# A new prelude, a deeper stream of loads, and ScalarE copies as seeds of PSUM in place of additions on VectorE

## The chip, the cores and the metric

The kernel runs on one core of a Trainium2 chip. The metric is the device time of one execution in microseconds (us). Times are the median of several runs; a profile is one more execution, recorded by the hardware profiler.

The core has TensorE (PE, matrix products out of SBUF into PSUM; its weight loads are listed as PEld), VectorE (DVE), ScalarE (ACT), GpSimd (POOL), SyncE (SP, which here only issues DMAs) and 16 DMA engines that all queues share. Each engine works through its own instructions in order.

## The reference

One layer of a bidirectional encoder on 512 rows of width 2048, in float32. What matters here is its beginning:

```python
mod = silu(c) @ w_ada + b_ada                    # w_ada: 2048 x 6144
shift, scale, gate = split(mod, 3)
h = rms_norm(x, g) * (1 + scale) + shift         # x: 512 x 2048
proj = h @ w_in                                  # w_in: 2048 x 7168
q_a, k_a, v_a, z_a, q_r, k_r, v_r, z_r = split(proj, ...)
# dilated-window attention (8 heads) on the first four,
# two-way retention (4 heads) on the last four,
# each gated by silu(z), put side by side as y
out = rms_norm(x + gate * (y @ w_out), final_gain)
```

So the product with `w_in` needs h, and a k-tile of h (128 of its 2048 columns) needs the shift and the scale of these 128 columns, and with them 256 columns of all 2048 rows of `w_ada`.

## The kernel before

**Products.** Each float32 operand is split into a high and a low part. For a weight, `conv` (L536 to L552) does it: ScalarE casts the loaded tile `raw` to `whi` (L543), VectorE subtracts to get `wlo` (L544). Each product is then three on TensorE (`mm3`, L85 and L87): high by high, and the two mixed ones.

**The prelude** (L89 to L455) loads, all through SyncE's queue, the columns of `w_ada` for the first k-tile (`araw`, 512-byte rows), then `x` in eight halves of a row tile. VectorE multiplies the 16 pieces of `w_ada` by the entries of silu(c) and adds them (L279, L281). ScalarE squares x (L302), GpSimd takes the power -1/2 of the mean (L319), and x is turned by TensorE and scaled by its rows' factors either in the product itself (L351, with the factors on a diagonal `dg`, L327) or on the way out of PSUM (L373, with the factors spread over all partitions in `rsb`). `psk` holds k-tile 0 of the turned x, from which h of k-tile 0 is made (L385, L386, L389). "Pinned" instructions (`pin`) keep the traced order on their engine; the others are ordered by a planner that goes by the traced order and by when it reckons their inputs to be there.

**Phase 1** (L873 to L974) projects 13 units of 256 columns of `w_in`, with the 16 k-tiles in chunks of 1, 2, 2, 3, 4 and 4 (`CHUNKS`): all units for one chunk, then all for the next, while the modulation of the next chunk is computed. Units 0 and 1 stay in PSUM (`pp`, pool `psP`) through all chunks. The other eleven ("loose") get two banks from a pool of three (`psA`, tile `pw`) for a chunk and are then added to sums in SBUF (`acc`): a copy on ScalarE the first time (L939), an addition on VectorE afterwards (L941). The order of units is turned round from chunk to chunk, and the last loose unit of a chunk stays in PSUM for the next one.

**The modulation of the next chunk** (`ada_pieces`, L188 to L267): steps that load rows of `w_ada` into one of `AR` = 3 buffers `araw` and, `AR` steps later, multiply and add them: the first product on ScalarE (L212), the other 15 on VectorE (L216). Then the sums over the partitions (L230, or turned by TensorE and summed on ScalarE, L244 and L249), shift and scale (L234 to L253), and h: `make_h` on ScalarE (L168, L172) and `make_hl` on VectorE (L181). These steps are put between the items of phase 1 by `plan` (L894), `LAG` = 3 items after the start of the chunk before.

**The stream** (`feed`, L592): an item is half a load of weights. Its load is issued (L564 or L623, buffers `raw`, `RAW` = 3) when it is fed; `LEAD` = 4 items later it is split, and `LOOK` = 2 items after that its products are issued.

The rest of the kernel (attention, retention, the other units, the output projection) isn't touched by the change.

Of the kernel before, what the change touches and what calls it, by code (L numbers as in the profile page):

```python
# [17 lines left out]
P = 128  # L18
D = 2048
# [28 lines left out]
AR = 3  # L48
# [3 lines left out]
def trunk_kernel(ctx, tc, x, c, norm_gain, w_ada, b_ada, w_in, w_out, dec_f, dec_b, final_gain, out):  # L52
# [51 lines left out]
    raw0 = []  # L104
    bg_row = const.tile([48, P], F32, name="bg_row")
    for n in range(4):
        raw = aap.tile([P, 1024], F32, tag="araw" if n < AR else "aacc", name="araw", bufs=AR if n < AR else None)
        rv = raw.rearrange("p (a b f) -> p a b f", a=4, b=2)
        for b in range(2):
            nc.sync.dma_start(  # L110
                rv[:, :, b],
                wa[n * 4 * P : (n + 1) * 4 * P, b * D : b * D + P].rearrange("(a p) f -> p a f", p=P),
            )
            if n + b == 0:
                nc.sync.dma_start(c_row, c.rearrange("b (k p) -> (b k) p", p=P))
        raw0.append(rv)
        if n == 1:
            nc.sync.dma_start(bg_row[0:32, :], b_ada[:, 0 : 2 * D].rearrange("b (k p) -> (b k) p", p=P))
            nc.sync.dma_start(bg_row[32:48, :], norm_gain.rearrange("b (k p) -> (b k) p", p=P))
    ssx = const.tile([P, NT, 2], F32, name="ssx")  # L120
    rsx = const.tile([P, NT], F32, name="rsx")
    xn = []
    for t in range(NT):
        xt = xp.tile([P, D], F32, name=f"xt{t}")
        for h in range(2):
            hs = slice(h * 1024, (h + 1) * 1024)
            nc.sync.dma_start(xt[:, hs], x2[t * P : (t + 1) * P, hs])
# [24 lines left out]
    # an engine keeps to the traced order of pinned instructions  # L152
# [120 lines left out]
    nc.vector.tensor_copy(bg, ps0[:, 64:112])
    nc.vector.tensor_scalar_add(bg[:, 16:32], bg[:, 16:32], 1.0)
    acc0 = [aap.tile([P, 2 * P], F32, tag="acc0", name="acc0") for _ in range(2)]
    for k in range(NK):
        rv, c1 = raw0[k // 4][:, k % 4], ct[:, k : k + 1]
        if k < 2:
            nc.vector.tensor_scalar_mul(acc0[k], rv, c1)  # L279
# [2 lines left out]
    rsb = aap.tile([P, S], F32, name="rsb", bufs=1)

    def sums0():
        psa = bank(psA, "psa")
        for i in range(2):
            for b in range(2):
# [11 lines left out]
    def squares(t, h):
        sq = xp.tile([P, 1024], F32, tag="sq", name="sq")  # L300
        v = xn[t][:, h * 1024 : (h + 1) * 1024]
        marks["sq"] = pin(nc.scalar.activation(sq, v, AF.Square, accum_out=ssx[:, t, h : h + 1]))  # L302

    mss = {}

    def half_root(t):
        ms = mss[t] = small.tile([P, 2], F32, tag="ms2", name="ms2", bufs=2)
        pin(nc.vector.tensor_scalar(ms[:, 0:1], ssx[:, t, 0:1], 1.0 / D, EPS, op0=ALU.mult, op1=ALU.add))

    def roots(t):  # L310
        if t not in mss:
            half_root(t)
        ms = mss[t]
        pin(
            nc.vector.scalar_tensor_tensor(
                ms[:, 1:2], ssx[:, t, 1:2], 1.0 / D, ms[:, 0:1], op0=ALU.mult, op1=ALU.add
            )
        )
        nc.gpsimd.tensor_tensor(rsx[:, t : t + 1], ms[:, 1:2], mhalf[:, 0:1], op=ALU.pow)  # L319

    # the rows' factors: on a diagonal, then on every partition
    dgs = {}
    psbs = {}

    def diagonal(t):
        dg = dgs[t] = xp.tile([P, P], F32, tag="dg", name="dg", bufs=2)
        marks["dg"] = pin(nc.vector.tensor_scalar_mul(dg, ident, rsx[:, t : t + 1]))  # L327
# [979 lines left out]
```

## Time and profile before

| | us |
|---|---|
| median of 3 runs | 971.41 |
| the three runs | 969.67, 971.41, 974.25 |
| span of the profiled execution | 971.6 |

The span runs from the first instruction to the last; of the profiled execution no other time is given. The product of k-tile 0 starts at 28.75 us of the span, chunk 1 at 53.18, chunk 2 at 93.12, chunk 3 at 133.99, chunk 4 at 194.87, chunk 5 at 268.87.

How to read it: a row of a group of instructions gives line, engine, operation, the tile written and the tiles read, the shape, the count, the busy time in us with the mean of one in ns, and the idle time of the engine just before them with what ended most of it. In a timeline the row starts with the start time and the length, and the idle time stands in brackets. In the list of waits: who waited for whom, the total in us, how often, and the longest. Busy time of TensorE isn't progress: a product of 512 columns that ends 0.39 us after its start follows the one before after 0.23 us, so products per stretch say more than the busy share.

### The profile page before, as it was taken

To read this page: it belongs to the slowest core of one execution; us is meant where nothing else is said; L and a number is where in the kernel's file an instruction comes from. 1 tells how busy PE (TensorE), PEld (TensorE's weight loads), DVE (VectorE), ACT (ScalarE), POOL (GpSimd) and SP (SyncE) were. 2 spreads that over 40 slices of the span, in tenths; PEclk is the share of its full clock that TensorE was granted. 3 is DMA by queue.
4 is the path that set the end of the run, shared out by engine and by line. 5 is a ranking of instruction groups with operands and counts; after the bars stand their busy time and mean duration, and the time that the engine had idled before them with its cause. 6 is when DMAs were issued, how large, how long until landed. Compare 5 with 4: busy or idle time off the path is not lost.

```text
span 971.6 us, 14377 instructions
## 1 busy us (share of the span) xinstructions
PE 941.5 (97%) x5556; PEld 820.4 (84%) x5556; DVE 618.0 (64%) x1101; ACT 376.5 (39%) x732; POOL 10.6 (1%) x22
## 2 busy tenths in 40 slices
PE   5989898999999999999999999999999999999996
PEld 4877687788988888988998899988899988888896
DVE  5879978977968786664555556745534382535444
ACT  3824242525235555444343232422333372333321
POOL 0000000000000000000000000000000000000001
PEclk9989999999999999999999999999999999999999
DMA  9786878763552222212224525425322148233304
GB/s 316 232 260 209 270 250 290 266 202 99 183 179 84 65 66 66 65 45 88 84 69 161 186 66 184 143 88 198 126 63 90 57 159 283 86 128 134 109 1 173
DMA packets 109715, 141.49 MB, mean 146 GB/s; under 512 B 6024, under 2 KB 78408, under 8 KB 109648
## 3 DMA queue, kind: packets, MB, share of 16 engines
q1 hardware_dynamic: 108496, 138.49, 43.4%
q10 hardware_dynamic: 1152, 2.10, 0.6%
q8 instruction: 43, 0.70, 0.3%
q14 instruction: 24, 0.20, 0.1%
HBM read 136.36 MB, written 4.20 MB: 145 GB/s over the span
## 4 chain that ended last, share of the span: by engine, by line
PE 89%; DMA 5%; DVE 3%; issue 2%; SPq 1%; ACT 0%; POOLq 0%; POOL 0%; DVEq 0%; ACTq 0%
PE pp L87 26%; PE pw L87 14%; PE pp L85 13%; PE po L87 12%; PE pw L85 7%; PE po L85 6%; PE op L87 3%; PE sp L87 2%; DMA raw<-in_w_in_dram 2%; DMA araw<-in_w_ada_dram 2%; PE op L85 2%; PE tp L770 1%; DVE aacc L216 1%; PE sp L85 1%; DMA xt<-in_x_dram 1%
## 5 line engine op out<-in xcount | busy, mean ns | idle before, releaser
L543 ACT CAST whi<-raw 128x512 fp32r<-128x512 f32 (+1 forms) x289 | 174.9, 606 | 435.8 <-PE pp L87 204.9
L544 DVE TENSOR_TENSOR wlo<-raw,whi 128x512 fp32r<-128x512 f32 (+1 forms) x289 | 193.9, 672 | 209.6 <-ACT whi L543 205.3
L85 PE MATMUL pp<-whi,hh 128*128 128x256 f32 x576 | 162.4, 282 | 0.0
L87 PE MATMUL pp<-wlo,hh 128*128 128x256 f32 x576 | 161.9, 281 | 0.0
L87 PE MATMUL pp<-whi,hl 128*128 128x256 f32 x576 | 161.5, 280 | 0.0
L85 PEld LDWEIGHTS pp<-whi,hh 128*128 128x128 f32 x576 | 108.5, 188 | 2.5 <-ACT sc L839 1.7
L87 PEld LDWEIGHTS pp<-wlo,hh 128*128 128x128 f32 x576 | 108.5, 188 | 1.0 <-DVE wlo L544 0.2
L87 PEld LDWEIGHTS pp<-whi,hl 128*128 128x128 f32 x576 | 108.5, 188 | 0.0
L85 PE MATMUL pw<-hh,whi 128*128 128x512 f32 x256 | 102.5, 401 | 3.6 <-DVE acc L941 3.6
L85 PE MATMUL pp<-hh,whi 128*128 128x512 f32 x256 | 102.7, 403 | 3.3 <-ACT hh L168 2.9
L87 PE MATMUL pp<-hh,wlo 128*128 128x512 f32 x256 | 102.1, 399 | 0.0
L87 PE MATMUL pp<-hl,whi 128*128 128x512 f32 x256 | 101.6, 397 | 0.0
L87 PE MATMUL pw<-hh,wlo 128*128 128x512 f32 x256 | 101.3, 396 | 0.0
L87 PE MATMUL pw<-hl,whi 128*128 128x512 f32 x256 | 101.1, 395 | 0.1
L87 PE MATMUL po<-wlo,yh 128*128 128x512 f32 (+1 forms) x252 | 92.6, 367 | 0.0
L85 PE MATMUL po<-whi,yh 128*128 128x512 f32 (+1 forms) x252 | 92.5, 367 | 0.0
L87 PE MATMUL po<-whi,yl 128*128 128x512 f32 (+1 forms) x252 | 92.5, 367 | 0.0
L216 DVE SCALAR_TENSOR_TENSOR aacc<-araw,ct,aacc 128x512 f32<-128x512 f32 (+2 forms) x75 | 76.1, 1014 | 10.8 <-DMA araw<-in_w_ada_dram 10.3
L941 DVE TENSOR_TENSOR acc<-acc,pw 128x512 f32<-128x512 f32 x100 | 66.3, 682 | 7.8 <-PE pw L87 7.3
L991 DVE SCALAR_TENSOR_TENSOR gacc<-graw,ct,gacc 128x512 f32<-128x512 f32 x60 | 45.0, 750 | 38.3 <-DMA graw<-in_w_ada_dram 38.0
L85 PEld LDWEIGHTS pp<-hh,whi 128*128 128x128 f32 x256 | 48.8, 191 | 16.7 <-ACT hh L168 3.0
L85 PEld LDWEIGHTS pw<-hh,whi 128*128 128x128 f32 x256 | 48.1, 188 | 17.3 <-DVE acc L941 5.7
(232 smaller groups left out, 1555.3 us busy)
## 6 DMA issues: line engine op xcount, KB each, us to landing
raw<-in_w_in_dram SPq DMA_DIRECT2D x94, 512.0 KB, 3.5
araw<-in_w_ada_dram SPq DMA_DIRECT2D x32, 512.0 KB, 5.5
graw<-in_w_ada_dram SPq DMA_DIRECT2D x64, 256.0 KB, 2.9
raw<-in_w_out_dram SPq DMA_DIRECT2D x32, 512.0 KB, 3.5
araw<-in_w_ada_dram SPq DMA_DIRECT2D x40, 256.0 KB, 3.7
raw<-in_w_in_dram SPq DMA_DIRECT2D x16, 384.0 KB, 5.4
araw<-in_w_ada_dram SPq DMA_DIRECT2D x16, 384.0 KB, 3.7
xt<-in_x_dram SPq DMA_DIRECT2D x8, 512.0 KB, 8.6
```

Of the source, the lines that this page charges most:

```text
L85: nc.tensor.matmul(o, lh, rh, start=start, stop=False, skip_group_check=True)
L87: nc.tensor.matmul(o, a, b, start=False, stop=stop and b is (rl if swap else rh), skip_group_check=True)
L216: ins = nc.vector.scalar_tensor_tensor(acc[:, :, :n], rv[:, a], ct[:, kr + a : kr + a + 1], acc[:, :, :n], op0=ALU.mult, op1=ALU.add,)
L543: c1 = nc.scalar.copy(dh, src)
L544: c2 = nc.vector.tensor_tensor(dl, src, f32(dh), op=ALU.subtract)
L770: nc.tensor.transpose(tp_[:, j * P : (j + 1) * P], pt[:, j * P : (j + 1) * P], ident)
L941: nc.vector.tensor_tensor(accs[u][i], accs[u][i], ps[i], op=ALU.add)
L991: nc.vector.scalar_tensor_tensor(st["acc"], raw, ct[:, kr : kr + 1], st["acc"], op0=ALU.mult, op1=ALU.add)
```

## The change

- **Loads of the prelude.** `x` is loaded by ScalarE's queue, four whole row tiles, first of all. SyncE loads `c` and the first k-tile's columns of `w_ada` in four pieces. The bias rows go through GpSimd's queue.
- **Modulation of k-tile 0.** Its sums are 32 TensorE products of a 128x128 piece of `w_ada` by one column of silu(c) (`sums0`), in place of VectorE products and additions.
- **x.** One half of the squares of a row tile on ScalarE (`squares_a`), the other on VectorE (`squares`); VectorE scales x in place (`scaled`); TensorE turns the scaled tile (`turned`); ScalarE or VectorE copies it out of PSUM (`evacuated`). The last row tile is turned late, and copied out between the first items of the stream. More warming products for TensorE (`WARM`, 10 + 3 + 3 in place of 9 + 1).
- **Buffers and leads.** `AR` 3 to 6. In chunks 0 to 3, every other load of `w_in` goes to one of three more buffers (`raw1`), and an item is split 8 items after its load (`LEAD1`) in place of 4; the loads of chunk 0 are all issued before its first item.
- **Seeds.** In chunks 1, 2 and 3 (`SEEDED`), five of the eleven loose units (`loose[1:-1:2]`) get their sum so far copied into their two PSUM banks by ScalarE before their products, the products add to it, and ScalarE copies the result back to `acc`: no addition on VectorE.

```diff
+SEEDED = 1, 2, 3
-WARM = 9
-WARM2 = 1
-LATE_AT = 7, 8
+WARM = 10, 3, 3
-RAW, WB, LOOK, LEAD, EB, YB = 3, 3, 2, 4, 1, 22
+RAW, RAW1, WB, LOOK, LEAD, LEAD1, EB, YB = 3, 3, 3, 2, 4, 8, 1, 22
-AR = 3
+AR = 6
@@ raw_tile
+    early = {"on": True, "n": 0}
     def raw_tile():
+        early["n"] += 1
+        if early["on"] and early["n"] % 2 == 0:
+            return aap.tile([P, 1024], F32, tag="raw1", name="raw1", bufs=RAW1)
         return wp.tile([P, 1024], F32, tag="raw", name="raw", bufs=RAW)
@@ loads of the prelude
+    for t in range(NT):
+        nc.scalar.dma_start(xn[t], x2[t * P : (t + 1) * P, :])
+    nc.sync.dma_start(c_row, c.rearrange("b (k p) -> (b k) p", p=P))
+    for i in range(2):
+        for b in range(2):
+            load0(nc.sync, b, i)
+    nc.gpsimd.dma_start(bg_row[0:32, :], b_ada[:, 0 : 2 * D].rearrange("b (k p) -> (b k) p", p=P))
+    nc.gpsimd.dma_start(bg_row[32:48, :], norm_gain.rearrange("b (k p) -> (b k) p", p=P))
@@ modulation of k-tile 0, squares and scaling
+    def sums0(b, i):
+        for a in range(8 * i, 8 * i + 8):
+            pin(
                 nc.tensor.matmul(
+                    psa[:, b : b + 1], raw0[b][:, a, :], ct[:, a : a + 1],
+                    start=a + b == 0, stop=a == NK - 1, skip_group_check=True,
                 )
+            )
+    def squares(t):
+        sd = aap.tile([P, 1024], F32, tag="aacc", name="sqd")
+        v = xn[t][:, 1024:2048]
+        pin(nc.vector.tensor_tensor_reduce(sd, v, v, 1.0 / D, EPS, ALU.mult, ALU.add, ssx[:, t, 1:2]))
...
+    def scaled(t, a, b):
+        v = xn[t][:, a:b]
+        marks["sc"] = pin(nc.vector.tensor_scalar_mul(v, v, rsx[:, t : t + 1]))
@@ order of the prelude
+    warm(WARM[0])
+    squares_a(0)
+    for t in range(NT):
+        squares(t)
+        if t:
+            evacuated(t - 1, 0, dve)
+        if t == 1:
+            turn_rows()
+        if t == 3:
+            psk3 = bank(psM, "psk3")
+            sums0(0, 0)
+            sums0(1, 0)
+        scaled(t, 0, P)
+        k0_part(t)
+        if t == 3:
+            break
+        scaled(t, P, 1024)
+        turned(t, 0)
+        turned(t, 1)
+        scaled(t, 1024, D)
+        turned(t, 2)
+        turned(t, 3)
+        if t < 2:
+            warm(WARM[1 + t])
+        squares_a(t + 1)
+        for b in range(1, 4):
+            evacuated(t, b, act)
+    sums0(0, 1)
+    sums0(1, 1)
+    scaled(3, P, 1024)
+    shift_scale0()
...
+    late = [lambda b=b: evacuated(3, b, act if b % 2 else dve) for b in range(4)]
@@ feed
-        if len(loaded) > (LEAD if item is not None else 0):
+        lead = LEAD1 if early["on"] else LEAD
+        while len(loaded) > (lead if item is not None else 0):
             it = loaded.pop(0)
             pending.append((it, it["conv"]()))
+            if item is None:
+                break
@@ phase 1
-    for i, f in zip(LATE_AT, late):
-        agenda.setdefault(i, []).append(f)
+    for i, f in enumerate(late):
+        agenda.setdefault(LEAD1 + LOOK + i, []).append(f)
+        early["on"] = ci < len(CHUNKS) - 2
-            def post(ps, u=u, ev=ev, lastc=lastc, keep_now=keep_now):
+            def post(ps, u=u, ev=ev, lastc=lastc, keep_now=keep_now, seed=ci in SEEDED and u in loose[1:-1:2]):
-                        if u not in begun:
+                        if u not in begun or seed:
                             nc.scalar.copy(accs[u][i], ps[i])
                         else:
                             nc.vector.tensor_tensor(accs[u][i], accs[u][i], ps[i], op=ALU.add)
+            seed = ci in SEEDED and u in loose[1:-1:2]
+            def seeded(u=u):
+                ps = [bank(psA, "pw") for _ in range(2)]
+                for i in range(2):
+                    nc.scalar.copy(ps[i], accs[u][i])
+                return ps
+            if seed:
+                pss, start, stop = seeded, False, True
+            elif u < N_PERSIST:
-            if u < N_PERSIST:
                 pss = lambda u=u: persist[u]
+        if ci == 0:
+            for it in items:
+                it["load"]()
```

More of the change, by code (lines that the diff above doesn't have):

```diff
@@ L282, in trunk_kernel, with turn_rows @@
[L282 to L287, printed above, removed]
+    def turn_rows():
+        pin(nc.tensor.transpose(ps0[:, 64:112], bg_row, ident[0:48, 0:48]))
+        pin(nc.vector.tensor_copy(bg, ps0[:, 64:112]))
+        pin(nc.vector.tensor_scalar_add(bg[:, 16:32], bg[:, 16:32], 1.0))
+    psa = bank(psA, "psa")
+    psk = bank(psA, "psk")
+    def sums0(b, i):
+        for a in range(8 * i, 8 * i + 8):
+            pin(
@@ L299, in squares @@
[L299 to L313, printed above, removed]
+                    psa[:, b : b + 1], raw0[b][:, a, :], ct[:, a : a + 1],
@@ L317, in roots @@
             )
         )
[L319 to L327, printed above, removed]
-    def spread(t):
-        psb = bank(psA, "psb")[:, 0:P]
-        pin(nc.tensor.matmul(psb, ones, dgs[t], start=True, stop=True))
-        psbs[t] = psb
-    def spread_out(t):
-        pin(nc.vector.tensor_copy(rsb[:, t * P : (t + 1) * P], psbs[t]))
+        nc.gpsimd.tensor_tensor(rsx[:, t : t + 1], ms, mhalf[:, 0:1], op=ALU.pow)
@@ L343, in turned, with evacuated @@
             pin(nc.tensor.transpose(ps[:, j * P : (j + 1) * P], xn[t][:, k * P : (k + 1) * P], ident))
-    def turned_scaled(t, b):
-        ps = psx[t, b] = bank(psP, "psx")
-        for j in range(4):
-            k = 4 * b + j
-            pin(
-                nc.tensor.matmul(
-                    ps[:, j * P : (j + 1) * P], xn[t][:, k * P : (k + 1) * P], dgs[t], start=True, stop=True
-                )
-            )
-    def pieces(b):
+    def evacuated(t, b, eng):
         for i, g in enumerate(groups):
@@ L389, in h0_low @@
         marks["hl"] = pin(nc.vector.tensor_tensor(hl[0][:, cols], tmp0[:, cols], f32(hh[0][:, cols]), op=ALU.subtract))
-    for _ in range(WARM):
-        pin(nc.tensor.matmul(ps0[:, 128:256], ones, ident, start=True, stop=True))
-    turned(0, 0)
-    turned(0, 1)
-    for _ in range(WARM2):
-        pin(nc.tensor.matmul(ps0[:, 128:256], ones, ident, start=True, stop=True))
-    turned(0, 3)
-    for t in range(2):
-        squares(t, 0)
-        squares(t, 1)
-    roots(0)
-    psa = sums0()
@@ L429, in trunk_kernel, with warm @@
-    marks["conv1"] = [marks["sq"]]
-    psk3 = bank(psM, "psk3")
-    turned_scaled(2, 2)
-    turned_scaled(2, 3)
-    roots(3)
-    scaled(2, 0)
-    turned(3, 0)
-    diagonal(3)
-    marks["conv1"].append(marks["dg"])
-    k0_part(3)
+    def warm(n):
+        for _ in range(n):
+            pin(nc.tensor.matmul(ps0[:, 128:256], ones, ident, start=True, stop=True))
+    warm(WARM[0])
[4 more added lines that the diff above has]
+            evacuated(t - 1, 0, dve)
+        if t == 1:
+            turn_rows()
[18 more added lines that the diff above has]
+            evacuated(t, b, act)
@@ L446, in trunk_kernel @@
     h0_low(B)
-    spread(3)
-    turned(3, 2)
-    evacuated(2, 3)
-    turned(3, 3)
-    spread_out(3)
-    scaled(3, 0)
-    scaled(3, 1)
-    late = [lambda b=b: scaled(3, b) for b in (2, 3)]
+    scaled(3, 1024, D)
+    for b in range(4):
+        turned(3, b, lambda ins: ins)
+    late = [lambda b=b: evacuated(3, b, act if b % 2 else dve) for b in range(4)]
     x_scope.close()
```

112 lines of the change are left out of this document (28 added, 84 removed).

## The prediction

> **What bounds the kernel now.** I read the page first, then the busy time by stage, then the waits of TensorE, then the timeline around the longest of them.
>
> ```profile
> span 971.6 us, 14377 instructions
> ...
> PE 941.5 (97%) x5556; PEld 820.4 (84%) x5556; DVE 618.0 (64%) x1101; ACT 376.5 (39%) x732; POOL 10.6 (1%) x22
> ```
>
> TensorE (PE) is busy for 941.5 of 971.6 us, so nothing that leaves its products alone can win more than the lost time on TensorE. The busy time by stage, cut at the first product of each chunk of phase 1, shows where that lies (columns: stretch, its length, then busy time and count of PE, PEld, DVE, ACT, POOL, the granted clock, the DMA share and GB/s):
>
> ```profile
> 0.00:28.75 28.75, 17.48 (x114) 15.72 (x115) 15.73 (x54) 13.76 (x25) 3.14 (x13) 0.94 0.92 311
> 28.75:53.18 24.43, 21.00 (x113) 17.05 (x113) 20.66 (x43) 17.70 (x35) 0.00 (x0) 0.98 0.77 243
> 53.18:93.12 39.94, 39.93 (x196) 33.53 (x197) 35.72 (x58) 14.74 (x30) 0.00 (x0) 0.93 0.69 219
> 93.12:133.99 40.87, 37.93 (x199) 31.55 (x198) 38.29 (x56) 14.70 (x33) 0.00 (x0) 1.00 0.78 258
> 133.99:194.87 60.88, 57.15 (x298) 47.05 (x296) 52.16 (x74) 22.18 (x52) 0.00 (x0) 1.00 0.81 277
> 194.87:268.87 74.00, 74.00 (x394) 62.84 (x392) 57.78 (x107) 25.77 (x55) 0.88 (x1) 1.00 0.51 161
> 180.00:200.00 20.00, 20.00 (x87) 16.09 (x86) 18.90 (x27) 7.41 (x14) 0.00 (x0) 1.00 0.79 255
> ```
>
> The last row is a stretch without loss: 87 products of 512 columns in 20 us, 0.230 us each. A chunk of nk k-tiles has 13 units x 2 x 3 x nk = 78 nk of them: 17.9 us for chunk 0, 35.9 for chunks 1 and 2, 53.8 for chunk 3. The stretches last 24.43, 39.94, 40.87 and 60.88, so they lose 6.5, 4.0, 5.0 and 7.1 us. From chunk 4 on nothing is lost. With the 28.75 us before the first product, that is all this change can touch.
>
> ```profile
> PE pw L85 <- DVE acc L941: 4.7, 6, 1.7
> PE pp L85 <- ACT hh L168: 2.9, 1, 2.9
> PE psm L244 <- ACT junk L249: 1.5, 1, 1.5
> ...
> 51.80 0.62 ACT L543 CAST whi<-raw 128x512 fp32r<-128x512 f32 x1 [3.42 <-DMA raw<-in_w_in_dram]
> ...
> 53.18 1.22 PE L85 MATMUL pp<-hh,whi 128*128 128x512 f32 x2 [2.95 <-ACT hh L168]
> ...
> 52.00:56.00 4.00, 2.82 (x9) 2.44 (x10) 3.45 (x6) 2.44 (x4) 0.00 (x0) 0.52 0.88 291
> 56.00:60.00 4.00, 4.00 (x13) 3.12 (x13) 1.62 (x3) 0.33 (x1) 0.00 (x0) 0.63 0.63 173
> ```
>
> Three causes. Chunk 1 starts late: ScalarE stands 3.42 us at a cast for a late w_in load, h of chunk 1 is queued behind it, and TensorE waits 2.95 us. After that wait the granted clock is 0.52 and 0.63 for two rows: most of chunk 1's 4.0 us is that. In chunks 2 and 3 TensorE waits for VectorE's additions (L941) to free a PSUM bank.
>
> ```profile
> L941 DVE TENSOR_TENSOR acc<-acc,pw 128x512 f32<-128x512 f32 x58 | 37.9, 682 | 1.3 <-PE pw L87 1.0
> L216 DVE SCALAR_TENSOR_TENSOR aacc<-araw,ct,aacc 128x1024 f32<-128x1024 f32 x25 | 32.0, 1281 | 7.4 <-DMA araw<-in_w_ada_dram 7.2
> L544 DVE TENSOR_TENSOR wlo<-raw,whi 128x512 fp32r<-128x512 f32 x44 | 30.1, 686 | 5.1 <-ACT whi L543 5.0
> L216 DVE SCALAR_TENSOR_TENSOR aacc<-araw,ct,aacc 128x512 f32<-128x512 f32 x30 | 22.4, 747 | 1.0 <-DMA araw<-in_w_ada_dram 0.8
> L216 DVE SCALAR_TENSOR_TENSOR aacc<-araw,ct,aacc 128x768 f32<-128x768 f32 x15 | 15.2, 1014 | 0.2 <-DMA araw<-in_w_ada_dram 0.2
> L544 DVE TENSOR_TENSOR wlo<-raw,whi 128x256 fp32r<-128x256 f32 x18 | 7.6, 420 | 1.4 <-ACT whi L543 1.3
> L181 DVE TENSOR_TENSOR hl<-ht,hh 128x512 fp32r<-128x512 f32 x11 | 7.3, 686 | 0.3 <-ACT ht L172 0.2
> ```
>
> VectorE's work for chunk 2 is 20 additions x 0.682, 15 modulation products for chunk 3 x 1.014, 13 low parts x 0.686 and 3 of h x 0.686: 39.8 us against 35.9 us of TensorE. For chunk 3: 20 x 0.682 + 15 x 1.281 + 13 x (0.686 + 0.420) + 4 x 0.686 = 50.0 against 53.8, with 7.2 us of standing at w_ada loads on top. VectorE is the bound of these two chunks, partly by work and partly by loads that come late.
>
> **The change part by part.** *Seeding.* In chunks 1, 2 and 3 five units each (every other of the eleven loose ones) drop two additions: 10 x 0.682 = 6.8 us off VectorE per chunk, leaving 33.0 of 35.9 in chunk 2 and 43.2 of 53.8 in chunk 3. ScalarE gets 20 copies per chunk, ten out of PSUM and ten into it.
>
> ```profile
> L939 ACT COPY acc<-pw 128x512 f32<-128x512 f32 x22 | 12.6, 590 | 2.7 <-PE pw L87 2.0
> ...
> ACT aacc L212 <- DMA araw<-in_w_ada_dram: 8.3, 2, 4.7
> ...
> 113.51 0.62 ACT L543 CAST whi<-raw 128x512 fp32r<-128x512 f32 x1 [3.00 <-DVE aacc L216]
> ```
>
> Out of PSUM one takes 0.590. Into PSUM no row exists; the nearest are 0.590 and the cast's 0.62, the bounds 0.4 and 0.8, and I take 0.6. That is 11.9 us more on an engine that is busy 14.7 of 40.87 us in chunk 2: hidden by its idle time. The new wait: a seed needs a bank that the unit before last has left (three banks, two per unit), then the first product needs the seed. Queued behind a seed on ScalarE are casts for later items and h of the next chunk.
>
> *Loads.* Six buffers instead of three for w_ada (AR), three more for w_in (RAW1), and loads issued 8 items ahead instead of 4 in chunks 0 to 3. This acts on the 7.2 us of VectorE, the 8.3 us of ScalarE and the 3.42 us shown above. There is room: chunk 0 moves 243 GB/s, chunk 1 219, where 311 was had before.
>
> *Prelude.* x goes to ScalarE's queue at once; SyncE loses eight issues and starts w_in and w_ada earlier; the modulation of k-tile 0 moves from 16 VectorE products to 32 small TensorE products; x is scaled in place before it is turned, and the squares are shared between ScalarE and VectorE.
>
> ```profile
> 0.74 0.44 SPq L110 DMA_DIRECT2D araw<-in_w_ada_dram  x1
> 5.56 0.35 DVE L279 TENSOR_SCALAR acc<-araw,ct 128x256 f32<-128x256 f32 x1 [0.35 <-DMA araw<-in_w_ada_dram]
> 6.47 6.34 SPq L127 DMA_DIRECT2D xt<-in_x_dram  x8
> 13.77 1.06 ACT L302 ACTIVATE sq<-xt 128x1024 f32<-128x1024 f32 x1 [9.27 <-DMA xt<-in_x_dram]
> ...
> 4.00:8.00 4.00, 0.49 (x2) 0.35 (x2) 0.96 (x4) 0.18 (x1) 0.00 (x0) 1.00 1.06 289
> 12.00:16.00 4.00, 2.15 (x18) 1.96 (x18) 2.42 (x7) 2.04 (x3) 0.00 (x0) 1.00 1.01 407
> ```
>
> The DMA engines are full in both rows, at 289 GB/s in w_ada's short rows and 407 in x, so a second queue adds no bandwidth. The first 256 KB piece, 0.9 us of transport, came 4.8 us after its issue: 3.9 us fixed. Then w_ada's columns (2.1 MB, 7.3 us) and x (4.2 MB, 10.3 us) are both in at 0.74 + 3.9 + 17.6 = 22.2 us in whatever order; x's first tile can be in at 7.2.
>
> By the Trainium skill, "DMA: Bandwidth & Descriptors", section "Issuing engines are not separate DMA queues", DMAs of several engines interleave on the same 16, and a second issuer saves little but issue time; by its section on queues and rings, an engine turns between queues packet by packet. By that rule x's long rows get past w_ada's 512-byte ones, and the modulation is the last to arrive. The trace of before loads through one queue alone and can't show it.
>
> ```profile
> L319 POOL TENSOR_TENSOR rsx<-ms,mhalf 128x1 f32<-128x1 f32 x4 | 2.2, 553 | 23.5 <-DVE ms L315 23.5
> L373 DVE TENSOR_TENSOR xT<-psx,rsb 128x128 f32<-128x128 f32 x6 | 1.6, 281 | 0.0
> L373 DVE TENSOR_TENSOR xT<-psx,rsb 128x256 f32<-128x256 f32 x3 | 1.3, 422 | 0.1
> L327 DVE TENSOR_SCALAR dg<-ident,rsx 128x128 f32<-128x128 f32 x4 | 1.1, 287 | 0.7 <-POOL rsx L319 0.4
> L279 DVE TENSOR_SCALAR acc<-araw,ct 128x256 f32<-128x256 f32 x2 | 0.7, 349 | 0.4 <-DMA araw<-in_w_ada_dram 0.4
> L385 ACT ACTIVATE hh<-psk,sv,av 128x384 fp32r<-128x384 f32 x1 | 0.7, 679 | 0.0
> ```
>
> VectorE now carries the prelude. Per tile of x: half the squares (no row; 1.06 on ScalarE and 1.28 of L216 at this width bound it, I take 1.2), scaling 2048 columns in three pieces (0.349 - 0.287 = 0.062 per 128 columns, so 16 x 0.062 + 3 x 0.225 = 1.7), two pieces out of PSUM (0.42 + 0.28), a small sum: 3.8. Four tiles less the unfinished scaling of the last (1.3), plus the first wait for the power on POOL (0.55 + 0.2), from 7.2: 21.9. Then 0.66 of scaling, 0.5 of shift and scale, and h in two parts on ScalarE (0.68 + about 0.45): 24.3. If x's last tile lands at 22.2 instead, 1.25 + 0.55 + 0.3 + 0.3 + 0.45 and hops of 0.8 follow: 25.8. First product: 25.2 for 28.75. ScalarE's four issues of x (6.34 / 8 = 0.8 each) put its first work 3 us later, and only the 32 small products wait for that; the two bias rows move to POOL's queue and are wanted at tile 1; both cost nothing while x arrives, and 1 to 3 us if TensorE came to wait for them. TensorE's extra (six more warming products) fits in its idle time: busy 17.48 of 28.75.
>
> *Chunk 1.* Chunk 0 needs 17.9 us and about 1.9 for the last tile's transposes: done at 45.0. Before chunk 1 come 12.7 MB (x, 6.3 of w_ada, 1.7 + 0.5 of w_in); at the first stretch's 311 GB/s 40.8 us, landed by 43, then two products of 0.75, the sums and h: 46.5. First product of chunk 1 at 46.5 for 53.18: **-6.7 us**.
>
> *Chunks 1 to 3.* Of 4.0 + 5.0 + 7.1 = 16.1 us lost I keep 2.2 (some 18 transposes of modulation sums, TensorE's own work) and 3.0 of waits (some seeds, a late load): **-10.9 us**.
>
> *Sum*: 971.6 - 6.7 - 10.9 = 954.0. The profiled span is 0.2 us from the median of 971.41, so it serves for both.
>
> By the Trainium skill, "TensorE: Matmul & The Clock Gate", section on the HAM clock gate, about 3.4 us without enough activity halve the clock until a busy window has passed. The rows after 52.00 agree. By that rule a quiet prelude would hand chunk 0 a halved clock, worth some 2 us; I leave that to the range.
>
> **The rivals.** *x is late.* If the queues share by bytes, SyncE's w_in and w_ada loads delay x: 4.2 MB of others run beside it (14 us at about 300 GB/s) and its last tile lands near 29, first product near 32. For: every load of SyncE is now free to start early. Against: x is issued first. Chunk 1 then starts at 52: -1.2 - 10.9, 959.5.
>
> *The seeds bring nothing.* If late loads alone hold VectorE back, the buffers do all; if work does, chunk 2's excess of 3.9 us stays where seeding fails to remove it: 958.
>
> *The loads stay late.* Chunk 3 already runs DMA at 0.81. If deeper buffers only lengthen the queue, chunks 1 to 3 lose as before: 971.6 - 6.7 = 965.
>
> *The seeds stand in the path* (slower). Last addition 0.682, then two seeds of 0.6: 1.9 us between the end of one unit and the first product of the next if ScalarE reaches them late, as it would while it stands 4.7 us at a w_ada load or 3.0 us at VectorE (rows above). In 15 units that is 28 us: 954 + 28 = 982. It decides against the change from 17.6 / 15 = 1.2 us per seeded unit. Against: a unit of chunk 1 or 2 lasts 12 x 0.23 = 2.8 us, and the bank for its first half is free for one unit's time.
>
> **How the numbers follow.** Forecast 954.0 (own range 948 to 959): 0.58. x late 0.12, seeds bring nothing 0.12, loads late 0.11, seeds in the path 0.07. The range leaves out the last one and half of the loads' case: 948 to 966. The low end has the first product at 24, chunk 1 right behind chunk 0 and one wait less per chunk. A measurement tells about 0.5% (4.9 us) from no change: faster 0.85, same 0.08 (the loads' case and its neighbours), slower 0.07.
>
> **What would show it.** Right: the first L85 product near 25 and chunk 1's near 46; no granted clock under 0.9 between 45 and 60; VectorE's additions in phase 1 down by 30 and ScalarE's copies up by 60; no wait of TensorE over 1 us between 46 and 180. Wrong: TensorE waiting for ScalarE's copies into `pw` (seeds in the path), ScalarE or VectorE standing at `araw` loads of 4 us (loads late), the last squares waiting for x after 24 us (x late).

## The result, and the profile after

The changed kernel is slower: 987.18 us (median of 4 runs, 985.98 to 987.80) beside 972.83 us for the kernel before on the same chip; the ratio on record, which isn't quite the quotient of the two medians, is 1.0155, 95% interval 1.0123 to 1.0187. The forecast was 954.0 (948 to 966): wrong sign, and outside the range.

The head of the page of the changed kernel:

```profile
span 984.7 us, 14429 instructions
...
PE 946.2 (96%) x5596; PEld 826.3 (84%) x5596; DVE 598.2 (61%) x1052; ACT 405.7 (41%) x795; POOL 11.8 (1%) x24
```

Its busy time by stage, cut at the first product of each chunk as before (columns as before: length, busy time and count of the five engines, granted clock, DMA share, GB/s), with two rows from the end of the prelude:

```profile
0.00:43.09 43.09, 23.79 (x154) 22.55 (x154) 14.52 (x40) 12.08 (x26) 4.35 (x15) 0.89 0.78 260
43.09:66.69 23.60, 22.80 (x112) 18.88 (x113) 20.44 (x40) 18.40 (x38) 0.00 (x0) 0.90 0.72 225
66.69:107.57 40.88, 37.80 (x197) 31.25 (x196) 37.95 (x56) 24.64 (x49) 0.00 (x0) 1.00 0.91 311
107.57:148.60 41.03, 37.87 (x200) 31.31 (x198) 36.57 (x47) 26.60 (x54) 0.00 (x0) 1.00 0.94 318
148.60:209.23 60.63, 57.05 (x302) 47.50 (x301) 40.36 (x59) 31.92 (x78) 0.00 (x0) 1.00 0.54 180
...
36.00:40.00 4.00, 4.00 (x20) 4.00 (x21) 0.00 (x0) 0.00 (x0) 0.00 (x0) 0.50 0.00 0
40.00:44.00 4.00, 3.56 (x14) 3.07 (x15) 2.17 (x7) 1.98 (x5) 0.00 (x0) 0.50 0.00 0
```

The reader is to see three things. The first product comes at 43.09 us where it came at 28.75: these 14.3 us are more than the whole difference of the spans, 984.7 - 971.6 = 13.1. Chunks 1 to 3 last 40.88 + 41.03 + 60.63 = 142.5 us, where they lasted 39.94 + 40.87 + 60.88 = 141.7: the 10.9 us that were to be won there are not won. And in the last two rows the weight loads of TensorE are busy for all, or three quarters, of the time, while the clock is halved and no DMA moves.

What became of the first 43 us stands in its timeline:

```profile
0.74 14.28 ACTq L122 DMA_DIRECT2D xt<-in_x_dram  x4
...
1.20 11.42 SPq L116 DMA_DIRECT2D raw<-in_w_ada_dram  x4
...
15.04 1.28 ACT L146 ACT_TABLE_LOAD   x1 [15.04 <-DMA raw<-in_w_ada_dram]
...
17.05 0.17 DVE L149 TENSOR_TENSOR ct<-ps,ce 128x16 f32<-128x16 f32 x1
17.14 1.22 DVE L306 CUSTOM_DVE_ANT_0 sqd<-xt 128x1024 f32<-128x1024 f32 x1
...
30.48 3.63 PE L287 MATMUL psa<-ct,raw 128*128 128x1 f32 x32
...
34.23 6.83 PE L287 MATMUL psa<-ct,raw 128*128 128x1 f32 x32
...
41.09 0.16 DVE L294 TENSOR_TENSOR sv<-psa,bg 128x1 f32<-128x1 f32 x1 [8.81 <-PE psa L287]
```

The DMA queues of the same kernel from 7 to 11 us (packets, MB, share of the 16 engines; q10 is ScalarE's queue with x, q1 SyncE's with `w_ada`):

```profile
q10 hardware_dynamic: 199, 1.50, 92.2%
q1 hardware_dynamic: 199, 0.10, 9.0%
```

ScalarE's four issues of x last from 0.74 to 15.02 us. The program gives each load a completion semaphore, and the fourth load of x shares one with the second piece of `w_ada`, so its issue waits for that piece. The piece is slow: from 7 to 11 us the queues move 199 packets each, nearly all of x's (183) rows of 8 KB and all of `w_ada`'s rows of 512 bytes, so x gets 1.50 of 1.61 MB and `w_ada` 0.10. ScalarE works in order: the table for its first function, silu(c), the squares and with them VectorE's first work come behind the issue, at 15 to 17 us (in the run e1 below, with x on SyncE's queue, ScalarE's first square starts at 6.15). Later VectorE waits 8.81 us for the sums of k-tile 0 on TensorE.

The longest of its waits of TensorE, over the whole span:

```profile
PE ps L354 <- DVE ct L149: 13.7, 1, 13.7
PE pw L90 <- ACT pw L906: 8.1, 6, 2.3
...
PE pw L90 <- ACT whi L486: 1.5, 1, 1.5
```

Its groups of additions and of copies into PSUM:

```profile
L890 DVE TENSOR_TENSOR acc<-acc,pw 128x512 f32<-128x512 f32 x70 | 46.7, 681 | 8.0 <-PE pw L92 7.7
...
L906 ACT COPY pw<-acc 128x512 f32<-128x512 f32 x30 | 17.7, 593 | 6.7 <-DVE acc L890 6.4
```

One seed in its timeline:

```profile
87.33 1.02 DVE L218 SCALAR_TENSOR_TENSOR aacc<-araw,ct,aacc 128x768 f32<-128x768 f32 x1 [1.72 <-DMA araw<-in_w_ada_dram]
...
88.27 0.68 DVE L890 TENSOR_TENSOR acc<-acc,pw 128x512 f32<-128x512 f32 x1
...
88.98 1.11 ACT L906 COPY pw<-acc 128x512 f32<-128x512 f32 x2 [0.23 <-DVE acc L890]
89.62 0.19 PEld L90 LDWEIGHTS pw<-hh,whi 128*128 128x128 f32 x1 [2.70 <-ACT pw L906]
89.62 0.50 PE L90 MATMUL pw<-hh,whi 128*128 128x512 f32 x1 [2.27 <-ACT pw L906]
```

VectorE's additions of whole banks fell from 100 to 70 as announced, and a seed takes 0.593 us where I had assumed 0.6. But TensorE now waits 8.1 us for seeds, where it had waited 4.7 us for additions. In chunks 1 to 3 the two kernels lose as much in different ways: before, TensorE's clock was at 0.93 in chunk 1, now it is at 1.00 and the seeds' waits have taken the place. The timeline shows one such wait from end to end: VectorE stands at a late load of `w_ada`, its addition for the unit before is late by that, the addition frees the bank for the seed, and the first product waits for the seed.

### The profile page after: what moved, and what is told of

Its sections match the earlier page's. It is cut to its first block, busy times and chain, and to the rows that moved or that the text cites. A ratio compares the mean times of both kernels' runs of the same rounds, so it can differ in the third digit from the quotient of the medians.

```text
span 984.7 us, 14429 instructions
## 1 busy us (share of the span) xinstructions
PE 946.2 (96%) x5596; PEld 826.3 (84%) x5596; DVE 598.2 (61%) x1052; ACT 405.7 (41%) x795; POOL 11.8 (1%) x24
## 4 chain that ended last, share of the span: by engine, by line
PE 86%; DMA 5%; DVE 4%; issue 2%; ACT 1%; SPq 0%; POOL 0%; POOLq 0%; DVEq 0%; ACTq 0%
PE pp L92 25%; PE pp L90 13%; PE pw L92 12%; PE po L92 12%; PE pw L90 6%; PE po L90 6%; DMA araw<-in_w_ada_dram 4%; PE op L92 3%; PE sp L92 2%; PE op L90 2%; PE tp L718 1%; DVE aacc L218 1%; DMA raw<-in_w_ada_dram 1%; PE sp L90 1%; PE psa L287 1%
## 5 line engine op out<-in xcount | busy, mean ns | idle before, releaser
L90 PE MATMUL pp<-whi,hh 128*128 128x256 f32 x576 | 162.4, 282 | 0.0
L90 PE MATMUL pw<-hh,whi 128*128 128x512 f32 x256 | 104.0, 406 | 10.0 <-ACT pw L906 7.3
L90 PEld LDWEIGHTS pp<-whi,hh 128*128 128x128 f32 x576 | 108.4, 188 | 2.5 <-ACT sc L787 1.7
L90 PE MATMUL pp<-hh,whi 128*128 128x512 f32 x256 | 101.2, 397 | 0.4 <-DVE kl L618 0.4
L90 PE MATMUL po<-whi,yh 128*128 128x512 f32 (+1 forms) x252 | 92.5, 367 | 0.0
L90 PEld LDWEIGHTS pw<-hh,whi 128*128 128x128 f32 x256 | 48.5, 189 | 24.7 <-ACT pw L906 9.7
L90 PEld LDWEIGHTS pp<-hh,whi 128*128 128x128 f32 x256 | 48.1, 188 | 13.5 <-ACT vh L616 0.9
L92 PEld LDWEIGHTS pw<-hh,wlo 128*128 128x128 f32 x256 | 48.5, 190 | 11.9
```

Source lines behind the costliest of these rows:

```text
L90: nc.tensor.matmul(o, lh, rh, start=start, stop=False, skip_group_check=True)
L92: nc.tensor.matmul(o, a, b, start=False, stop=stop and b is (rl if swap else rh), skip_group_check=True)
```

## The experiments

All ratios are to the kernel before on the same chip, with their 95% intervals. "First product" is the start of chunk 0. The kernel before took 971.1 to 973.1 us from chip to chip, so times of two runs are compared by their ratios. The table gives all 15 runs; a stage is that of one profiled execution, and chunks 1 to 3 spread from 139.9 to 142.5 us among kernels of equal time (e11, e14, e15). The first product spreads too: with the prelude of before unchanged (before, e5, e6, e9, e10, e11, e14, e15) it lies between 26.8 and 28.8 us and chunk 1 starts between 49.6 and 53.2. The profile of before, from which the prediction counts, is the latest of these eight in both.

| run | us | ratio | first product | chunks 1 to 3 | chunk 5 |
|---|---|---|---|---|---|
| before | 972.8 | 1 | 28.8 | 141.7 | 91.6 |
| after | 987.2 | 1.0155 [1.0123, 1.0187] | 43.1 | 142.5 | 91.7 |
| e1 x on SyncE | 978.9 | 1.0080 [1.0048, 1.0111] | 30.6 | 141.0 | 93.3 |
| e2 sums early | 984.8 | 1.0123 [1.0096, 1.0149] | 40.6 | 142.9 | 92.1 |
| e3 both | 978.9 | 1.0058 [1.0035, 1.0081] | 28.4 | 146.2 | 96.3 |
| e4 no seeds | 983.1 | 1.0103 [1.0074, 1.0131] | 43.2 | 134.2 | 92.8 |
| e5 seeds alone | 979.2 | 1.0066 [1.0046, 1.0086] | 27.5 | 150.6 | 91.6 |
| e6 loads alone | 970.7 | 0.9967 [0.9948, 0.9987] | 27.3 | 136.8 | 98.0 |
| e7 prelude alone | 987.3 | 1.0143 [1.0115, 1.0171] | 43.1 | 142.0 | 91.6 |
| e8 e3, no seeds | 971.0 | 0.9985 [0.9967, 1.0003] | 28.1 | 136.0 | 95.5 |
| e9 e6, gate held | 966.6 | 0.9947 [0.9929, 0.9965] | 27.1 | 138.4 | 91.6 |
| e10 e5, other bank | 978.0 | 1.0066 [1.0042, 1.0089] | 26.8 | 148.1 | 91.6 |
| e11 e10, no seeds | 972.0 | 1.0008 [0.9992, 1.0025] | 27.5 | 142.5 | 91.6 |
| e12 e8, wide sums | 966.6 | 0.9944 [0.9923, 0.9966] | 26.9 | 135.9 | 96.5 |
| e13 e12, gate held | 963.9 | 0.9925 [0.9905, 0.9945] | 26.4 | 136.8 | 91.6 |
| e14 copies, no wait | 970.9 | 0.9991 [0.9974, 1.0008] | 26.8 | 139.9 | 91.6 |
| e15 copies out | 970.7 | 1.0002 [0.9985, 1.0020] | 27.7 | 140.9 | 91.7 |

**The prelude.** e1 moves x to SyncE's queue, behind c and ahead of `w_ada`:

```diff
-    for t in range(NT):
-        nc.scalar.dma_start(xn[t], x2[t * P : (t + 1) * P, :])
     nc.sync.dma_start(c_row, c.rearrange("b (k p) -> (b k) p", p=P))
+    for t in range(NT):
+        nc.sync.dma_start(xn[t], x2[t * P : (t + 1) * P, :])
```

> The changed kernel, but x is loaded by SyncE's queue (after c, ahead of w_ada's columns), so that no load stands in ScalarE's stream. Theory A (the fourth x load of ScalarE's queue waits for a w_ada piece and holds ScalarE, and with it silu(c) and the squares, until 15.0 us): the first square starts near 7 to 8 instead of 16.4, the first product of chunk 0 comes 7 to 10 us earlier than 43.1, the time is 977 to 980. Theory B (transport of x and w_ada sets the end of the prelude): the first square comes earlier but the first product stays within 2 us of 43.1, the time within 3 us of 987.

e2 leaves x where it was and spreads the sums of the first three quarters over the tiles of x; e3 has both edits:

```diff
         if t == 3:
...
-            sums0(0, 0)
-            sums0(1, 0)
+            sums0(0, 1)
+            sums0(1, 1)
...
+        if t:
+            sums0(t - 1, 0)
```

> The changed kernel, but the 32 one-column products for the modulation of k-tile 0 are spread over the tiles of x instead of standing behind the last one. Theory C (these products, 3.6 us at full clock and 6.8 at half, lie on the path, and their low activity halves the clock before chunk 0): VectorE no longer waits 8.8 us for psa, the first product comes near 35 to 37, no halved clock between 34 and 47, the time 977 to 980. If only their place matters and not the clock: first product near 37 to 39 with the halved clock still there, 982 to 984.

> Both edits at once: x on SyncE's queue and the sums spread. Theories A and C together: the first product near 25 to 28, the time 966 to 971 (18 us less than the changed kernel, if the two gains add up). If transport is the bound (B): the first product not before 33, the time 975 or more.

In e1 the first work on x starts at 6.15 us instead of 16.42 and the first product comes at 30.63, 12.5 us earlier. e1 moves the issue and also puts all of x ahead of `w_ada`; but in the changed kernel no work on x waits for a load once ScalarE is free, so the stalled issue is the main part of the 12.5. From e1's timeline:

```profile
0.74 1.28 ACT L146 ACT_TABLE_LOAD   x1 [0.74 <-PEq L1258]
...
6.15 1.06 ACT L301 ACTIVATE sqa<-xt 128x1024 f32<-128x1024 f32 x1 [2.46 <-DMA xt<-in_x_dram]
```

And one stretch of e1, in the columns of the busy time by stage:

```profile
24.00:28.00 4.00, 4.00 (x22) 4.00 (x22) 0.00 (x0) 0.00 (x0) 0.00 (x0) 0.53 1.09 352
```

The medians differ by 8.3 us, the spans of the profiled executions by 11.4; chunks 4 and 5 give 2.6 us back. The stretch from 24 to 28 us has TensorE busy throughout at a clock of 0.53. e2 wins 2.5 us at the first product and misses both of its expectations (40.6 us, for 35 to 37 or 37 to 39). e3 brings it to 28.4, but not the time below e1's, and misses its 966 to 971: chunks 1 to 3 and chunk 5 give it back. That left three questions: why the clock is halved under a busy TensorE, what is late in chunk 5, and what the seeds cost.

e12 answers the first. On e8 (e3 without seeds), the sums take 64 equal columns of silu(c) in place of one:

```diff
+    ctw = xp.tile([P, NK, 64], F32, name="ctw")
+    nc.gpsimd.tensor_copy(ctw, ct.rearrange("p (k a) -> p k a", a=1).to_broadcast([P, NK, 64]))
...
-                    psa[:, b : b + 1], raw0[b][:, a, :], ct[:, a : a + 1],
+                    psa[:, b * 64 : (b + 1) * 64], raw0[b][:, a, :], ctw[:, a, :],
```

> The mended prelude without seeds, but each of the 32 products for the modulation of k-tile 0 multiplies 64 equal columns of silu(c) instead of one (a copy made by GpSimd). Theory G (one-column products load weights all the time but count as idle for the clock gate): the clock stays at 1.0 through 23 to 30 us, the last 48 records take 5.4 us instead of 6.8, chunk 0's first products 0.23 instead of 0.43 us apart, the first product at 26 to 27.2 and chunk 1 some 2 to 3 us earlier. Rival (the clock falls for another reason, or the wider products are slower themselves): halved clock as before near 23 to 30, first product at 28 or later.

The last 48 records of the sums in e3's timeline, with one column (each product leaves two records):

```profile
19.57 6.80 PE L287 MATMUL psa<-ct,raw 128*128 128x1 f32 x48
```

The same stretch as above in e3:

```profile
24.00:28.00 4.00, 4.00 (x20) 3.78 (x19) 0.89 (x4) 0.66 (x2) 0.00 (x0) 0.50 1.09 352
```

The same records in e12's timeline, with 64 columns:

```profile
19.84 5.47 PE L289 MATMUL psa<-ctw,raw 128*128 128x64 f32 x48
```

And the same stretch in e12:

```profile
24.00:28.00 4.00, 3.32 (x25) 2.89 (x25) 1.88 (x7) 1.83 (x4) 0.00 (x0) 1.00 1.09 352
```

Sixty-four times the columns take 5.47 us in place of 6.80, at a clock of 1.00 in place of 0.50. A row of one-column products loads weights all the time, and yet the clock falls. By the ratios e12 is some 4 us faster than e8; 1.9 us of that lie ahead of chunk 1.

**The three parts, each alone.** e4 is the changed kernel with `SEEDED = ()`; e5, e6 and e7 are the kernel before with the seeds, the deeper loads, or the new prelude alone. e8 is e3 without seeds.

> The changed kernel without seeds (the additions on VectorE again for all units, prelude, buffers and leads as changed). Theory D (the seeds are a new link in the chain from VectorE to TensorE and cost what they save): chunks 1 to 3 lose 9 to 12 us as with seeds, TensorE waiting for VectorE's additions in their place, the time within 3 us of 987. Theory E (the seeds are what holds TensorE, 8.1 us of its waits): 979 to 982. Theory F (the seeds save work of VectorE that would bind): 992 to 996.

> The kernel before with the seeds alone (old prelude, three w_ada buffers, lead of 4). Theory D' (a seed lengthens the chain from VectorE's addition to TensorE's next product by one ScalarE copy, and ties it to ScalarE's queue, wherever the loads stand): chunks 1 to 3 last 4 to 9 us longer than before (141.7 us from the first product of chunk 1 to that of chunk 4), time 977 to 982. Rival (the seeds cost only because the new prelude left the loads behind): chunks 1 to 3 within 2 us or shorter, time 966 to 974.

> The kernel before with the buffers and leads alone (six w_ada buffers, three more w_in buffers, lead of 8, chunk 0's loads at once; old prelude, no seeds). If the late loads were what chunks 1 to 3 lost, as the run without seeds says (134.2 us for the three against 141.7): first product still near 29, chunks 1 to 3 near 134, time 962 to 966. Rival (the gain there was only the calm of a late start, with the loads long under way): chunks 1 to 3 at 139 or more, time 969 to 973.

> The new prelude alone (no seeds, three w_ada buffers, w_in buffers and leads as before). If the prelude's cost is its own: first product near 43, chunks 1 to 3 near 141, time 985 to 988. If the deeper loads made part of it (SyncE's loads beside x): first product near 38 to 41, time 980 to 984.

> The mended prelude (x on SyncE's queue, sums spread) with the deeper loads and without seeds. Additive: the mended one with seeds took 978.9, leaving the seeds out gained 4.1 on the changed kernel and 8.4 in its chunks 1 to 3: 970 to 975, first product near 28.4, chunks 1 to 3 near 135 instead of 146. If the mended prelude's loss in chunks 1 to 3 comes from its loads: 976 or more.

The prelude alone costs 14.4 us and the seeds alone 6.3, and the loads alone win 2.2. Together that is +18.5; the change measured +14.4, so the parts don't quite add. Without seeds, chunks 1 to 3 last 134.2 us in the changed kernel, 8.3 less than with them, about the 8.1 us that TensorE waits for seeds there; in e5 seeds make them 8.9 longer than before. Chunks 4 and 5 take 2.5 us of e4's gain back, and its time, 983.1, fits none of its three theories. e6's time is that of its rival, 969 to 973. It also shows where the gain of 4.9 us in chunks 1 to 3 goes: chunk 5 takes 98.0 us in place of 91.6. In e6's timeline:

```profile
280.61 0.75 DVE L1005 SCALAR_TENSOR_TENSOR gacc<-graw,ct,gacc 128x512 f32<-128x512 f32 x1 [2.23 <-DMA graw<-in_w_ada_dram]
...
281.88 1.28 DVE L952 TENSOR_TENSOR acc<-acc,pw 128x512 f32<-128x512 f32 x2
...
282.62 0.80 PE L90 MATMUL pw<-hh,whi 128*128 128x512 f32 x1 [2.93 <-DVE acc L952]
```

And the stretch that follows in e6:

```profile
284.00:288.00 4.00, 4.00 (x11) 3.06 (x10) 1.85 (x3) 0.89 (x2) 0.00 (x0) 0.50 0.35 102
```

VectorE stands 2.23 us at a load of the output gate's columns, work that nobody needs yet. The additions of phase 1 are queued behind it, TensorE waits 2.93 us, and after that the clock is halved. e9 is e6 with the gate's first product on VectorE held until phase 1's last addition; e13 is the same in e12:

```diff
-                            nc.vector.tensor_tensor(accs[u][i], accs[u][i], ps[i], op=ALU.add)
+                            marks["acc"] = nc.vector.tensor_tensor(accs[u][i], accs[u][i], ps[i], op=ALU.add)
...
-                nc.vector.tensor_scalar_mul(st["acc"], raw, ct[:, 0:1])
+                first = nc.vector.tensor_scalar_mul(st["acc"], raw, ct[:, 0:1])
+                if h == 0:
+                    after(first, marks["acc"])
```

> The kernel before with the deeper loads alone (as in the run of loads alone), and the gate's products on VectorE held back until the last addition of phase 1. In the run of loads alone chunk 5 lasted 98.0 us against 91.6: VectorE stood 2.2 us at a gate load with phase 1's addition behind it, TensorE 2.9 us, and the granted clock was halved for 6.8 us. If that is the loss: chunk 5 at 91 to 93, chunks 1 to 3 near 137, time 963 to 967. Rival (the gate's work only moves its waits to a later place): time 969 to 973.

> The after-kernel without seeds, with x on SyncE's queue behind c, the sums of k-tile 0 spread over x's tiles with 64 equal columns, and the gate's first product on VectorE held until phase 1's last addition. If the gate's products in VectorE's queue are what made chunk 5 last 96.5 us in the run with wide sums (91.6 with additions on time), chunk 5 returns to 91.6 and the time is 961 to 963, the fastest of all; as in the run with held gate and loads alone, chunks 1 to 3 may give 1 to 2 us back (136 to 138). If chunk 5 was late for another reason it stays at 95 to 97 and the time at 966 to 967.

In both, chunk 5 is back at 91.6 us. e13 is 0.9 us above its expected 961 to 963 and the fastest of all, 0.9925 (0.9905 to 0.9945) of the kernel before. e9, with the old prelude, is at 0.9947 (0.9929 to 0.9965): the intervals overlap, so these runs don't clearly show that the mended prelude is worth anything beside the old one.

**Why the seeds cost.** A seed does three things that an addition doesn't: it needs an empty bank before the unit's products, it puts 20 copies per chunk on ScalarE, and its copy out waits on ScalarE for the unit's last product. e10 takes the second bank of seeded units from another pool (as far as is known, part of the seeded units' sums so far is left out of its result, so it stands here for its time alone); e11 is the same choice of banks without seeds. e14 adds ScalarE's 20 copies per chunk to the kernel before as copies that wait neither for TensorE nor for a bank and are read by nobody; e15 has ScalarE copy those units' banks out and VectorE add the copy.

```diff
-                ps = [bank(psA, "pw") for _ in range(2)]
+                ps = [bank(psA, "pw"), bank(psM, "pw")]
```

```diff
+                    if seed:
+                        for i in range(2):
+                            nc.scalar.copy(aside(), far[i])
...
+                    if seed:
+                        for i in range(2):
+                            nc.scalar.copy(aside(), accs[u][i])
```

```diff
+                        elif seed:
+                            out = aside()
+                            nc.scalar.copy(out, ps[i])
+                            nc.vector.tensor_tensor(accs[u][i], accs[u][i], out, op=ALU.add)
```

> The seeds alone on the kernel before, but the second bank of a seeded unit is the one of the pool psM instead of a third of psA's three, so that each bank comes free earlier. Theory D' (VectorE's late addition, then one ScalarE copy, then the product, all inside the time of one unit): the wait of TensorE for the seeds falls from 3.9 us to under 2, chunks 1 to 3 from 150.6 to 141 to 145, time 970 to 974. Rival (the extra copies crowd ScalarE's queue, whichever bank they use): within 2 us of 979.

> The control of the run with the fourth bank: the kernel before, with the same bank of psM for the same units in chunks 1 to 3, and no seeds. If the bank alone is worth something: chunks 1 to 3 at 137 to 140, time 968 to 971; the seeds' own cost is then the difference of the two runs. If banks weren't short without seeds: within 2 us of 973.

> The kernel before with 20 more copies of ScalarE in each of chunks 1, 2 and 3, at the places where the seeds and their copies out stand, but from sums in SBUF into a tile that nobody reads; VectorE keeps its additions. None of them waits for TensorE or for a bank. Theory crowding: the seeds cost because 12 us more of copies per chunk stand ahead of the casts and h; then chunks 1 to 3 take 147 to 150 us (141.7 before) and the time is 977 to 979, as with the seeds alone. Theory blocking: the seeds cost because a copy that waits (for a bank, or for a unit's last product) holds all of ScalarE's later work, and the copies themselves fit in its idle time; then chunks 1 to 3 take 141 to 143 and the time is 971 to 974.

> The kernel before, where the seeded units' banks are copied out to SBUF by ScalarE (10 copies in each of chunks 1, 2 and 3) and VectorE adds the copy: no seed, but ScalarE waits for the unit's last product as it does for a seeded unit. Theory blocking by the copy out: chunks 1 to 3 take 145 to 149 us and the time is 975 to 978. If only the copy in (the seed, in front of a product) costs, chunks 1 to 3 take 141 to 143 and the time is 971 to 974.

The stages of chunks 1, 2 and 3 in e5:

```profile
51.24:93.13 41.89, 40.65 (x196) 33.16 (x197) 35.67 (x54) 25.09 (x50) 0.00 (x0) 0.93 0.83 271
93.13:136.88 43.75, 39.80 (x200) 32.87 (x199) 36.81 (x48) 25.14 (x53) 0.00 (x0) 0.96 0.85 288
136.88:201.85 64.97, 59.14 (x301) 48.58 (x300) 44.58 (x62) 33.14 (x79) 0.00 (x0) 0.97 0.67 225
```

TensorE's waits in e5, from 50 to 196 us:

```profile
PE pw L86 <- ACT pw L958: 3.9, 3, 2.0
...
PE pp L86 <- ACT hh L169: 2.4, 1, 2.4
```

The same list in e10:

```profile
PE pw L88 <- DVE wlo L545: 4.8, 4, 1.9
PE pp L86 <- ACT hh L169: 3.7, 1, 3.7
PE pw L86 <- ACT pw L958: 3.6, 2, 2.5
```

One wait of e10 in its timeline:

```profile
105.89 1.15 ACT L213 ACTIVATE aacc<-araw,ct 128x1024 f32<-128x1024 f32 x1 [4.00 <-DMA araw<-in_w_ada_dram]
...
108.41 1.12 ACT L958 COPY pw<-acc 128x512 f32<-128x512 f32 x2
...
109.58 0.79 PE L86 MATMUL pw<-hh,whi 128*128 128x512 f32 x1 [2.52 <-ACT pw L958]
```

The groups of the two kinds of copies that e14 adds:

```profile
L972 ACT COPY aside<-acc 128x512 f32<-128x512 f32 x30 | 18.6, 620 | 0.7
L951 ACT COPY aside<-acc 128x512 f32<-128x512 f32 x30 | 18.6, 619 | 1.8 <-DVE acc L948 1.3
```

e14 and e15 cost nothing (0.9991 and 1.0002, both intervals hold 1): neither the number of copies, 37 us of them in all, nor the wait of the copy out is the price, each taken by itself. My reading after e10, that ScalarE is crowded, falls with e14. e10 costs as much as e5 though its second bank is free, so the lack of a bank is not the price either, or not the only one. What is left is the copy in, which stands in the path ahead of the products and behind all of ScalarE's earlier work. The wait in e10's timeline shows it: ScalarE stands 4.00 us at a load of `w_ada`, then works without a break, the seed last, and TensorE waits 2.52 us for it.

Two more parts of the price stand in the traces. One is the clock: in e5 it is at 0.96 and 0.97 in chunks 2 and 3, where it was at 1.00 before. By the rows, my estimate for the 8.9 us is 4.3 of TensorE's idle time (11.0 for 6.7) and 3.8 of the lower clock (length times what is missing to 1.00: 6.6 for 2.8). e3's chunks 1 to 3, at 0.96, 0.96 and 0.97, are longer than those of the changed kernel at 1.00 in the same way.

The other is VectorE: in chunks 1 to 3 it stands 20.0 us at loads of `w_ada` in e5 and 19.2 in e10, beside 6.4 to 8.0 in before, e11, e14 and e15, and 10.5 and 10.6 us for ScalarE's casts beside 1.8 to 4.0; in the changed kernel 9.5 and 12.9, beside 0.2 and 0.9 without seeds (e4). So the additions and low parts of VectorE come late too (the 4.8 us of e10 are low parts made behind such modulation products), and with them the next seeds. How the price divides along this loop stays open; a seed copied a unit ahead, into banks of its own, was not tried.

## Why the prediction was wrong, point by point

**The step that failed: the prelude, 25.2 us predicted, 43.1 measured.** The 17.9 us between them, by the first products of the runs: 12.5 go with x on SyncE's queue (e1), 2.2 with the sums spread (e3), 0.3 without seeds (e8), 1.2 with wide sums and the full clock (e12), and 1.7 are left. Three statements stand behind these.
- "ScalarE's four issues of x ... put its first work 3 us later" and "cost nothing while x arrives, and 1 to 3 us if TensorE came to wait for them". The issues held ScalarE for 14.28 us, and all that needs silu(c), the squares too, came behind them. I had priced an issue by its length on SyncE (0.8 us) and did not ask what an issue can wait for. On SyncE, which does nothing but issue, such a wait has only later loads behind it.
- The 32 small products have no term in the sum; "fits in its idle time" speaks of the warming products alone. VectorE waited 8.8 us for them: the first 32 records took 3.63 us, the other 32, at the halved clock, 6.83.
- That w_ada's columns and x "are both in at 0.74 + 3.9 + 17.6 = 22.2 us in whatever order" came out near (x's last tile landed at 23.05 in the changed kernel), but what follows a landing was not in it. In e12, with the stall, the place and the clock mended, 48 of 64 records still ran from 19.8 to 25.3 us on TensorE and VectorE waited 2.25 us for them. The first product came at 26.9 (26.4 in e13), so the term 25.2 was short by 1.2 to 1.7 us. The "3.9 us fixed" were misread besides: the first piece landed 2.9 us after its issue, and the row at 5.56 waits for the second piece too.

By the Trainium skill, "DMA: Bandwidth & Descriptors", section "Queues, rings and completion order", a DMA engine turns between queues packet by packet. The trace agrees, 199 packets to 199 (a packet is one row in nearly all of them), and the prediction had drawn the right consequence for bytes (x passes `w_ada`) but not for ScalarE, which came to wait for the loser.

**Chunk 1, -6.7 us:** the start was wrong, and with it the term. Chunk 0 lasted 23.60 us after the first product, 21.3 predicted (46.5 - 25.2); in e12, at a clock of 1.00 where it was 0.90, it lasted 21.7, so some 1.9 us are the halved clock. The chain of loads, sums and h that was to set chunk 1's start didn't set it: no wait for its h is in the list, where before had one of 2.9 us, and TensorE is busy for 22.80 of the 23.60 us. Nor were all of the 6.7 us there to be won: with the prelude of before, chunk 1 starts at 49.6 to 53.2, in e12 at 48.5.

By the Trainium skill, "TensorE: Matmul & The Clock Gate", section on the HAM clock gate, the clock halves after an idle window of some 3.4 us and returns after a busy one. I had left "a quiet prelude" to the range. The prelude wasn't quiet: between 36 and 40 us TensorE counts as busy for 4.00 of 4.00 us at a clock of 0.50. What the gate counts isn't the busy time of the profile, as e3 and e12 show.

**Chunks 1 to 3, -10.9 us:** without seeds the changed kernel wins 7.5 of them (134.2): 2.3 in chunk 1, 0.9 in chunk 2 and 4.3 in chunk 3. Chunk 1 follows the clock, as predicted: about 37 to 38 us at 1.00 (e4, e12, and e14 with the old loads), 39.9 and 40.2 at 0.93 and 0.92 (before, and e9 with the deeper loads). VectorE's work for chunk 2 was put at 39.8 us, and without seeds chunk 2 lasted 40.0 in e4 and 40.8 to 42 in the others with deeper loads: work looks like the bound there, and the deeper loads bring nothing clear. Chunk 3 is where they help: 56.6 to 58.7 us without seeds, 59.2 to 62.4 with the old loads. What I did not see is that the deeper loads can make VectorE stand at the gate's loads with phase 1's additions behind it, at up to 6.4 us in chunk 5 (e6); with the old loads chunk 5 lasts 91.6 or 91.7 us in every run.

**The seeds, "hidden by its idle time":** the durations were right (0.593 for 0.6; 30 additions less, 60 copies more), the conclusion wrong. They cost 6.3 us alone, some 5 in the changed kernel (e4) and some 7 in the mended one (e3 beside e8, by the ratios). This was the rival "the seeds stand in the path", at a chance of 0.07; its mechanism is the row `PE pw L90 <- ACT pw L906`, at 8.1 us instead of its 28. That the rival's time of 982 lies near the measured 987 is chance: its 28 us were to come from seeds, the 14.4 came mostly from the prelude. I had dismissed it because "the bank for its first half is free for one unit's time". A free bank doesn't help: e10 had one for the second half and cost as much. Idle time in the mean (14.7 of 40.87 us busy) says nothing on whether an in-order engine is free at the one moment at which a product waits for it.

Of the signs listed, "no granted clock under 0.9 between 45 and 60" and "no wait of TensorE over 1 us" failed, as did the two first products (43.1 and 66.7); VectorE's 30 additions less and ScalarE's 60 copies more came true, and so did "TensorE waiting for ScalarE's copies into `pw`".

## What to carry to other kernels

Give a DMA that may wait to an engine with no computing behind it: here four issues on ScalarE cost what a semaphore waited for, 14.28 us, not their length. Before moving work off a busy engine, look at whether the new place is in front of a product: 30 additions behind the products cost less than 30 copies ahead of them, though the copies were shorter and their engine idler. Change one part at a time: a prelude that cost 14.4 us and seeds that cost 6.3 hid deeper loads that, with the gate's products held, make the kernel 0.53% faster than before (e9), and 0.75% with the mended prelude (e13). And take the start of a stage from more than one profile before counting a gain from it.

## What the runs showed of the hardware

- Products of one column against freshly loaded 128x128 weights keep TensorE busy by the profile but let the clock fall to 0.50 (e1, e2, e3 and after); with 64 columns it stayed at 1.00, and the row of products was shorter, 5.47 us for 6.80.
- With two queues at work the DMA engines moved as many packets of each, 199 and 199: 8 KB rows got 1.50 MB and 512-byte rows 0.10 MB in the same 4 us.
- A ScalarE copy of 128x512 took 0.593 us from SBUF into PSUM, 0.590 from PSUM into SBUF, and 0.62 from SBUF into SBUF (e14).
